# A decoder step's HGRN2 recurrence: the decayed q and k of a head multiplied in place, without a second buffer and the copies into it

## The chip, the cores and the metric

The kernel runs on one core of one Trainium2 chip. Its metric is the device time of one launch in microseconds (us). Of the kernel before, three runs are at hand: 1033.81, 1034.29 and 1036.57 us, median 1034.29. The engines of the core are named as the profile names them: PE (TensorE, matrix products; PEld is its loading of weights), DVE (VectorE), ACT (ScalarE), POOL (GpSimd) and SP (SyncE, which here only issues transfers). Each engine works through its own list of instructions in a fixed order, and semaphores make one engine wait for another.

## The reference

The kernel computes one inference step of a hybrid decoder layer of width 1024, for a prompt of 512 tokens and for 8 single new tokens (samples) with stored states, 520 columns in all. Cut to what matters here:

```
u = (rmsnorm(x) * (1 + scale1) + shift1) @ w_in          # eight parts of 1024 columns
q, f, i, og, xb, yb, ga, gb = split(u)
o_a = rmsnorm(HGRN2(silu(q), k, i, log f)) * silu(og)    # 8 heads, 128 x 128 state each
o_b = RGLRU(conv(xb)) * gelu(yb)
merged = sigmoid(ga) * (o_a @ w_branch_a) + sigmoid(gb) * (o_b @ w_branch_b)
x = x + gate1 * (merged @ w_out)
x = x + gate2 * (relu(h2 @ w_ff1) ** 2 @ w_ff2)          # and a last rmsnorm
```

HGRN2 is per head a recurrence S_t = diag(f_t) S_(t-1) + k_t v_t^T with the output o_t = S_t^T q_t. In chunks this is a triangular matrix A[t, s] = sum over the key dimension of q_t k_s times the product of the decays f between s and t, applied to v, plus the part that comes from the state at the start of the chunk. RG-LRU is an elementwise recurrence h_t = a_t h_(t-1) + sqrt(1 - a_t^2)(i_t x_t).

## The kernel before

**Products.** Every large product is done in three passes of a high and a low part: high weight by high activation, high weight by low activation, low weight by high activation (`products`, its matmul on L150). One group of 128 output columns over 1024 rows is 48 matmuls of 128x128 by 128x260. A weight tile of 512 KB comes in on SP's queue as `wst` (L102); ACT makes its high part `whi` (L111, a copy into another format) and DVE its low part `wlo`, the difference (L114). Both must be there before the group's products can be done.

**Order of the work.** A list of steps is built: for each head h of eight, `head(h)`, then two groups of the RG-LRU (`rg_x` after even heads, `rg_y` after odd ones); then the eight gate groups (`gate`, part 6 of `w_in`), in their middle `end_recurrences` and `begin_tail`, which load the heads' and the RG-LRU's results back from DRAM (`load_branches`, L877 and L882 on POOL's queue, with five buffers `t`; L200 on ACT and L201 on DVE split them into high and low parts `a` and `b`); then the products of branch a, the other gates, branch b, the output projection and the MLP. Some groups of the modulation product (L408, its result copied out by ACT at L413) are mixed in. The engines do not run these steps in program order: a planner lays out all instructions of the program over all engines with its own model of their durations, and what it decides is the order that each engine keeps. Waits follow from the data and from buffers that are used again. A few instructions, such as the reading of PSUM, have a higher priority.

**A head.** `head` makes f, k (L540) and q by activations, puts q*f, k and q into the three slots of a tile X of 128 x 3 x 520 (two buffers), and the samples' columns into `fkq`. `head_sample_v` transposes the samples' v on PE (L589), copies it (L591, DVE), writes it to DRAM (L593) and reads it back broadcast over all partitions as `vb` (L595, one buffer). `head_sample` updates the eight samples' states: ACT scales a state (L602) and DVE adds k v (L603, which waits for `vb`), for each sample; PE then makes the outputs (L609), and transposes them at L614, and DVE takes the wanted ones into `os` (L616).

**The levels of the recurrence.** `head_prompt` builds A for chunks of 128 tokens by doubling. L655 makes the diagonal products and those of the first level. A level of size b = 1, 2, 4, ..., 64 joins neighbouring blocks of b tokens: PE multiplies k of the left block by q of the right one (`block_level` L641 for b = 2 to 16, L673 for 32, L679 for 64), the result goes into the triangular matrix (`copy_predicated` into `a32`, L689, or ACT's copies into `at`), and then the q of every right block and the k of every left one, half of the columns of each, are multiplied by the block's decay (L681, 128 x 512 elements), while the decays of the level are multiplied in pairs for the next (L698). Before, L681 writes its half to a second tile Y, and a copy puts the halves that were not multiplied, as far as the other tile hasn't got them yet, there too (ACT L683 for b = 1, DVE L687 for all others); X and Y then change their names, and the next level works on the other tile.

After the last level, PE transposes k (L710) and multiplies it by v (L714), DVE chains the four chunk states (L716, L718), PE makes the outputs (L725, L727), ACT squares and sums them (L732), DVE makes the reciprocal root (L733 and L209 to L215), ACT scales (L737), PE transposes (L741), DVE multiplies by the gate (L743) and SP's queue stores the result (L744).

**RG-LRU.** `rg_x` makes gates with small block-diagonal products (L782, sigmoid L174). `rg_scans`, in odd heads for two units, is exp and tanh (L817, L818), square (L820), a combination on DVE (L821), sqrt on ACT (L824), then on DVE a product (L830) and the scan (L832). ACT loads a table before L817 and before L824.

Of the kernel before, what the change touches and what calls it, by code (L numbers as in the profile page):

```python
# [6 lines left out]
F32 = mybir.dt.float32  # L7
# [4 lines left out]
OP = mybir.AluOpType  # L12
# [6 lines left out]
T = L + NB  # L19
# [56 lines left out]
class Kernel:  # L76
# [541 lines left out]
    def head_prompt(self, h, f, X, q, v, og):  # L618
        nc = self.nc

        pv = self.pps.tile([128, 512], F32, name="ps")
        for c in range(NC):
            nc.tensor.transpose(pv[:, c * C:(c + 1) * C], v[:, c * C:(c + 1) * C], self.ident)
        vn = self.slot(self.hg, "g")
        nc.scalar.copy(vn[:, :L], pv)

        Y = self.hg.tile([128, 2, T], F32, name="Y", bufs=2)
        nc.vector.tensor_tensor(X[:, 0, :L], q[:, :L], f[:, :L], OP.mult)  # L630
        T_ = self.hg.tile([128, 508], F32, name="tb", bufs=2)
        tb, to = f[:, :L], 0
        a32 = self.hg.tile([128, NC, 32], F32, name="a32")
        at = self.at[h % 2]

        def block_level(x, y):
            p = self.pps.tile([128, 512], F32, name="ps")
            for c in range(NC):
                for j in range(4):
                    s = slice(c * C + 32 * j, c * C + 32 * j + 32)  # L640
                    nc.tensor.matmul(p[32 * j:32 * j + 32, c * 32:c * 32 + 32], x[:, s], y[:, s], start=True, stop=True)  # L641
            return p[:, :128].rearrange("p (c t) -> p c t", c=NC)

        def view(t, first_q, first_k, step, n, b):

            return bass.AP(tensor=t.tensor, offset=t.offset + first_q,
                           ap=[t.ap[0], [T + first_k - first_q, 2], [step, n], [1, b]])


        p = self.pps.tile([128, 512], F32, name="ps")  # L650
        for c in range(NC):
            for j in range(4):
                s = c * C + 32 * j
                o = p[32 * j:32 * j + 32, c * 64:c * 64 + 64].rearrange("p (x t) -> p x t", x=2)
                nc.tensor.matmul(o, X[:, 1, s:s + 32], X[:, 0::2, s:s + 32], start=True, stop=True)  # L655
        first = p[:, :256].rearrange("p (c x t) -> p c x t", c=NC, x=2)
        nc.vector.tensor_tensor(a32, first[:, :, 1], self.mdiag, OP.mult)
        b = 1
        while b < C:
            Q, K = X[:, 0], X[:, 1]  # L660

            n = L // (2 * b)
            fac = bass.AP(tensor=tb.tensor, offset=tb.offset, ap=[tb.ap[0], [1, 2], [2, n], [0, b]])
            if b == 1:
                p = first[:, :, 0]
            elif b <= 16:
                p = block_level(K, Q)
            elif b == 32:
                p = self.pps.tile([128, 512], F32, name="ps")
                for c in range(NC):  # L670
                    for j in (0, 64):
                        s = c * C + j
                        nc.tensor.matmul(p[j:j + 32, c * 32:c * 32 + 32], K[:, s:s + 32], Q[:, s + 32:s + 64],  # L673
                                         start=True, stop=True)
            else:
                p = self.pps.tile([128, 512], F32, name="ps")
                for c in range(NC):
                    s = c * C
                    nc.tensor.matmul(p[:64, c * 64:c * 64 + 64], K[:, s:s + 64], Q[:, s + 64:s + 128],  # L679
                                     start=True, stop=True)  # L680
            nc.vector.tensor_tensor(view(Y, b, 0, 2 * b, n, b), view(X, b, 0, 2 * b, n, b), fac, OP.mult)  # L681
            if b == 1:
                nc.scalar.copy(view(Y, 0, 1, 2, n, 1), view(X, 0, 1, 2, n, 1))  # L683
            else:

                h2 = b // 2
                nc.vector.tensor_copy(view(Y, h2, b, 2 * b, n, h2), view(X, h2, b, 2 * b, n, h2))  # L687
            if b <= 16:
                nc.vector.copy_predicated(a32, self.masks[b], p)  # L689
            elif b == 32:  # L690
                for j in (0, 64):
                    nc.scalar.copy(at[j:j + 32, :, j + 32:j + 64],
                                   p[j:j + 32, :128].rearrange("p (c t) -> p c t", c=NC))
            else:
                nc.scalar.copy(at[:64, :, 64:], p[:64, :256].rearrange("p (c t) -> p c t", c=NC))
            t2 = tb.rearrange("p (n two) -> p n two", two=2)
            tn = T_[:, to:to + n]
            nc.vector.tensor_tensor(tn, t2[:, :, 0], t2[:, :, 1], OP.mult)  # L698
            tb, to = tn, to + n
            X, Y = Y, X  # L700
            b *= 2
        Q, K = X[:, 0], X[:, 1]
        for j in range(0, 128, 32):
            nc.vector.tensor_copy(at[j:j + 32, :, j:j + 32], a32[j:j + 32])

        pk = self.ppt.tile([128, 512], F32, name="pt")
        for c in range(NC):
            nc.tensor.transpose(pk[:, c * C:(c + 1) * C], K[:, c * C:(c + 1) * C], self.ident)
        kn = self.slot(self.hg, "g")
        nc.scalar.copy(kn[:, :L], pk)  # L710
        pkv = self.ppt.tile([128, 512], F32, name="pt")
        for c in range(NC):
            s = slice(c * C, (c + 1) * C)
            nc.tensor.matmul(pkv[:, s], kn[:, s], vn[:, s], start=True, stop=True)  # L714
        S = self.slot(self.hg, "g")
        nc.vector.tensor_copy(S[:, :128], pkv[:, :128])  # L716
        for c in range(1, NC):
            nc.vector.scalar_tensor_tensor(S[:, c * 128:(c + 1) * 128], S[:, (c - 1) * 128:c * 128], tb[:, c:c + 1],  # L718
                                           pkv[:, c * 128:(c + 1) * 128], OP.mult, OP.add)
        nc.sync.dma_start(self.o["hgrn_p"][0, 0, h], S[:, 3 * 128:4 * 128])  # L720

        po = self.ppt.tile([128, 512], F32, name="pt")
        for c in range(NC):
            s = slice(c * C, (c + 1) * C)
            nc.tensor.matmul(po[:, s], at[:, c], vn[:, s], start=True, stop=c == 0)  # L725
            if c:
                nc.tensor.matmul(po[:, s], Q[:, s], S[:, (c - 1) * 128:c * 128], start=False, stop=True)  # L727
        o = self.slot(self.hg, "g")
        ss = self.sm.tile([128, 16], F32, name="ss")
        for c in range(NC):  # L730
            s = slice(c * C, (c + 1) * C)
            nc.scalar.activation(o[:, s], po[:, s], AF.Square, accum_out=ss[:, c:c + 1])  # L732
        nc.vector.tensor_scalar(ss[:, :NC], ss[:, :NC], 1.0 / 128, EPS, OP.mult, OP.add)  # L733
        ss = self.rsqrt_small(ss[:, :NC], NC)
        for c in range(NC):
            s = slice(c * C, (c + 1) * C)
            nc.scalar.activation(o[:, s], po[:, s], AF.Copy, scale=ss[:, c:c + 1])  # L737
        pt = self.ppt.tile([128, 512], F32, name="pt")
        for c in range(NC):
            s = slice(c * C, (c + 1) * C)  # L740
            nc.tensor.transpose(pt[:, s], o[:, s], self.ident)  # L741
        oa = og
        nc.vector.tensor_tensor(oa[:, :L], pt, og[:, :L], OP.mult)  # L743
        nc.sync.dma_start(self.oaT_d[h], oa[:, :L])  # L744
# [1128 lines left out]
```

## Time and profile before

| | |
|---|---|
| median of three runs | 1034.29 us (1033.81 to 1036.57) |
| profiled execution: span of its instructions | 1032.9 us |
| time outside the span, against the median | 1.4 us |
| PE busy | 1008.7 us, 98% |
| DVE busy | 691.4 us, 67%, 1520 instructions |
| ACT busy | 520.8 us, 50%, 988 instructions |
| heads and their recurrences | about 60 to 436 us of the span |
| first product of branch a | at 453.2 us |

The span is that of one profiled execution; no separate time of that execution is given beside it, so it is set against the median of the runs. A row of the timeline is: start in us, duration in us, engine, line and operation, output <- inputs, shape, and how many like it follow each other; in square brackets the idle time before it and what ended it. Rows that follow each other closely overlap somewhat, since an instruction's record reaches to the end of its last write; the pitch from start to start is then the shorter number. In the lists of groups the numbers behind the bar are the busy time in us, the mean of one in ns and the idle time before.

### The profile page before, as it was taken

To read this page: it belongs to the slowest core of one execution; us is meant where nothing else is said; L and a number is where in the kernel's file an instruction comes from. 1 tells how busy PE (TensorE), PEld (TensorE's weight loads), DVE (VectorE), ACT (ScalarE), POOL (GpSimd) and SP (SyncE) were. 2 spreads that over 40 slices of the span, in tenths; PEclk is the share of its full clock that TensorE was granted. 3 is DMA by queue.
4 is the path that set the end of the run, shared out by engine and by line. 5 is a ranking of instruction groups with operands and counts; after the bars stand their busy time and mean duration, and the time that the engine had idled before them with its cause. 6 is when DMAs were issued, how large, how long until landed. Compare 5 with 4: busy or idle time off the path is not lost. (4 is left out here: it accounts for less than half of the span.)

```text
span 1032.9 us, 23726 instructions
## 1 busy us (share of the span) xinstructions
PE 1008.7 (98%) x9756; PEld 967.5 (94%) x9756; DVE 691.4 (67%) x1520; ACT 520.8 (50%) x988; POOL 123.1 (12%) x228
## 2 busy tenths in 40 slices
PE   5999999999999999999999999999999999999997
PEld 2899999999999999988999999999999999999996
DVE  6787769595867869264233347667776776777685
ACT  4555744663575366342122235466555655655663
POOL 3200000000000000031000001011422231232140
PEclk9999999999999999999999999999999999999998
DMA  9673443434334324397555568322672474274242
GB/s 324 220 200 111 119 126 118 121 116 126 109 114 126 114 85 135 105 329 238 164 163 162 158 179 240 99 84 63 133 173 81 95 173 124 49 160 99 63 82 84
DMA packets 201822, 143.68 MB, mean 139 GB/s; under 512 B 6766, under 2 KB 189702, under 8 KB 201706
## 3 DMA queue, kind: packets, MB, share of 16 engines
q1 hardware_dynamic: 191090, 128.08, 41.6%
q0 software_dynamic: 10608, 14.05, 7.0%
q8 instruction: 76, 1.25, 0.5%
q14 instruction: 32, 0.26, 0.1%
q10 hardware_dynamic: 16, 0.03, 0.0%
HBM read 123.61 MB, written 11.26 MB: 131 GB/s over the span
## 5 line engine op out<-in xcount | busy, mean ns | idle before, releaser
L150 PE MATMUL mm<-h,whi 128*128 128x260 f32 (+1 forms) x2944 | 490.3, 286 | 0.0
L150 PEld LDWEIGHTS mm<-h,whi 128*128 128x128 f32 x2944 | 409.7, 189 | 5.2 <-issue 4.1
L150 PE MATMUL mm<-h,wlo 128*128 128x260 f32 x1472 | 305.2, 286 | 0.1
L111 ACT CAST whi<-wst 128x1024 fp32r<-128x1024 f32 x164 | 171.7, 1048 | 221.6 <-PE mm L150 182.0
L114 DVE TENSOR_TENSOR wlo<-wst,whi 128x1024 fp32r<-128x1024 f32 x164 | 200.3, 1223 | 102.0 <-ACT whi L111 100.3
L150 PEld LDWEIGHTS mm<-h,wlo 128*128 128x128 f32 x1472 | 230.5, 189 | 1.9 <-issue 0.8
L150 PE MATMUL mm<-a,whi 128*128 128x260 f32 x512 | 85.3, 286 | 0.0
L150 PEld LDWEIGHTS mm<-a,whi 128*128 128x128 f32 x512 | 70.5, 188 | 3.8 <-issue 3.3
L150 PE MATMUL mm<-a,wlo 128*128 128x260 f32 x256 | 51.7, 283 | 0.0
L877 POOL DMA_DIRECT2D t<-oaT_d x8 | 4.4, 552 | 387.8 <-ACT sq L750 378.1
L1270 DVE TENSOR_TENSOR f<-f 128x260 f32<-128x260 f32 x64 | 27.4, 428 | 27.6 <-ACT f L1265 26.9
L1259 ACT ACTIVATE ft<-ft,fsh 128x512 f32<-128x512 f32 (+2 forms) x36 | 24.0, 675 | 36.1 <-DVE ft L1256 36.1
L150 PE MATMUL mm<-b,whi 128*128 128x260 f32 x256 | 41.9, 286 | 0.0
L1262 POOL TENSOR_TENSOR ft<-ft,fsh 128x8 f32<-128x8 f32 x28 | 18.4, 657 | 187.3 <-DVE ft L1256 187.3
L150 PEld LDWEIGHTS mm<-a,wlo 128*128 128x128 f32 x256 | 39.5, 188 | 0.0
L150 PEld LDWEIGHTS mm<-b,whi 128*128 128x128 f32 x256 | 35.0, 188 | 3.3 <-issue 2.5
L1304 POOL DMA_DIRECT2D ma<-snap x28 | 26.8, 972 | 38.3 <-issue 29.2
L1286 POOL DMA_DIRECT2D ma<-snap x28 | 25.9, 926 | 36.7 <-DMA ma<-snap 25.1
L893 DVE TENSOR_TENSOR t<-mm,t 128x520 f32<-128x520 f32 x8 | 5.6, 700 | 36.5 <-PE mm L150 36.5
L1265 ACT ACTIVATE f<-ft 128x520 f32<-128x520 f32 (+1 forms) x36 | 20.7, 587 | 15.0 <-POOL ft L1263 13.0
L602 ACT ACTIVATE st<-st,fkq 128x128 f32<-128x128 f32 x64 | 20.2, 391 | 14.8 <-DVE fkq L581 12.5
L150 PE MATMUL mm<-b,wlo 128*128 128x260 f32 x128 | 25.9, 284 | 0.0
(579 smaller groups left out, 1940.9 us busy)
## 6 DMA issues: line engine op xcount, KB each, us to landing
wst<-in_w_in_dram SPq DMA_DIRECT2D x64, 512.0 KB
wst<-in_w_mod_dram SPq DMA_DIRECT2D x32, 512.0 KB
wst<-in_w_ff_dram SPq DMA_DIRECT2D x64, 256.0 KB
wst<-in_w_ff_dram SPq DMA_DIRECT2D x32, 512.0 KB
wm<-in_w_mod_dram SPq DMA_DIRECT2D x16, 512.0 KB
st<-in_state_hgrn_dram SPq DMA_DIRECT2D x8, 512.0 KB
vb<-vd SPq DMA_DIRECT2D x8, 512.0 KB
out_dram<-st SPq DMA_DIRECT2D x8, 512.0 KB
```

Source lines behind the costliest of these rows:

```text
L111: ins = self.nc.scalar.copy(hi, st)
L114: self.nc.vector.tensor_tensor(lo, st, hi.bitcast(F32), OP.subtract)
L150: self.last_product = self.nc.tensor.matmul(ps[s][:, :c.stop - c.start], x, y[:, c], start=first and n == 0, stop=last and n == 2)
L602: nc.scalar.activation(st[:, b], st[:, b], AF.Copy, scale=fkq[:, 0, b:b + 1])
L877: nc.gpsimd.dma_start(t[:, :L], self.oaT_d[h])
L893: self.nc.vector.tensor_tensor(self.two(s), ps, self.two(s), OP.mult)
L1259: nc.scalar.activation(t[:, :p], t[:, :p], AF.Relu, bias=sh[:, 0:1])
L1262: eng.tensor_tensor(t[:, p:], t[:, p:], sh[:, 1:9], OP.add)
L1265: nc.scalar.activation(f, self.two(self.ft)[:, a:a + n], AF.Square)
L1270: self.nc.vector.tensor_tensor(f[:, n], f[:, a], f[:, b], op)
L1286: nc.gpsimd.dma_start(x[1][:, b], v[:, :n], accum_op=OP.add)
L1304: nc.gpsimd.dma_start(x[t][:, a], s[p], accum_op=OP.add)
```

## The change

The tile Y goes. At each level the multiplication by the decays reads and writes the same half of X, and it is issued behind the step that takes the level's products into the triangular matrix instead of ahead of it. The copies of the other halves on ACT and DVE are not needed, since they never leave X, and X and Y no longer change places. Nothing else in the program text is different; the planner lays the changed program out anew.

```
-        Y = self.hg.tile([128, 2, T], F32, name="Y", bufs=2)
         nc.vector.tensor_tensor(X[:, 0, :L], q[:, :L], f[:, :L], OP.mult)
...
-            nc.vector.tensor_tensor(view(Y, b, 0, 2 * b, n, b), view(X, b, 0, 2 * b, n, b), fac, OP.mult)
-            if b == 1:
-                nc.scalar.copy(view(Y, 0, 1, 2, n, 1), view(X, 0, 1, 2, n, 1))
-            else:
-
-                h2 = b // 2
-                nc.vector.tensor_copy(view(Y, h2, b, 2 * b, n, h2), view(X, h2, b, 2 * b, n, h2))
             if b <= 16:
                 nc.vector.copy_predicated(a32, self.masks[b], p)
             elif b == 32:
...
             else:
                 nc.scalar.copy(at[:64, :, 64:], p[:64, :256].rearrange("p (c t) -> p c t", c=NC))
+            half = view(X, b, 0, 2 * b, n, b)
+            nc.vector.tensor_tensor(half, half, fac, OP.mult)
             t2 = tb.rearrange("p (n two) -> p n two", two=2)
             tn = T_[:, to:to + n]
             nc.vector.tensor_tensor(tn, t2[:, :, 0], t2[:, :, 1], OP.mult)
             tb, to = tn, to + n
-            X, Y = Y, X
             b *= 2
```

More of the change, by code (lines that the diff above doesn't have):

```diff
@@ L625, in head_prompt @@
         nc.scalar.copy(vn[:, :L], pv)
-        Y = self.hg.tile([128, 2, T], F32, name="Y", bufs=2)
         nc.vector.tensor_tensor(X[:, 0, :L], q[:, :L], f[:, :L], OP.mult)
@@ L680, in head_prompt @@
                                      start=True, stop=True)
[L681 to L687, printed above, removed]
             if b <= 16:
@@ L695, in head_prompt @@
                 nc.scalar.copy(at[:64, :, 64:], p[:64, :256].rearrange("p (c t) -> p c t", c=NC))
+            half = view(X, b, 0, 2 * b, n, b)
+            nc.vector.tensor_tensor(half, half, fac, OP.mult)
             t2 = tb.rearrange("p (n two) -> p n two", two=2)
@@ L699, in head_prompt @@
             tb, to = tn, to + n
-            X, Y = Y, X
             b *= 2
```

## Prediction

> **What bounds the kernel.** The page comes first: how busy each engine is and at what clock.
>
> ```profile
> span 1032.9 us, 23726 instructions
> PE 1008.7 (98%) x9756; PEld 967.5 (94%) x9756; DVE 691.4 (67%) x1520; ACT 520.8 (50%) x988; POOL 123.1 (12%) x228
> PEclk9999999999999999999999999999999999999998
> ```
>
> PE is the bound, at a full clock. Work that leaves DVE or ACT shortens nothing by itself; only a place where PE stands still can gain or lose. So the second view is a stretch with nothing but products (its columns: window, length, busy time of PE, PEld, DVE, ACT, POOL, mean clock, DMA share, GB/s), and the third the list of what PE and DVE waited for (total, times, longest).
>
> ```profile
> 650.00:675.00 25.00, 25.00 (x210) 25.00 (x209) 16.78 (x37) 11.50 (x17) 0.00 (x0) 1.00 0.30 85
> PE ps L641 <- DVE X L687: 1.5, 1, 1.5
> PE pt L614 <- DVE e L743: 1.2, 2, 1.0
> DVE st L603 <- DMA vb<-vd: 8.5, 6, 3.6
> ```
>
> 210 products in 25.00 us are 0.119 us each: PE's pace, by which I turn a count of products into time. In the heads' stage (60 to 430 us) PE lost only 2.7 us, in the two PE rows. One of them names a copy that this change removes, so I looked at the place, first as PE and then as DVE has it.
>
> ```profile
> 251.59 0.28 PE L150 MATMUL mm<-h,wlo 128*128 128x260 f32 x1
> 253.39 0.27 PE L641 MATMUL ps<-X 128*32 128x32 f32 x8 [1.52 <-DVE X L687]
> 253.89 0.44 PE L614 MATMUL pt<-ident,sev 128*128 128x128 f32 x2 [0.23 <-DVE e L743]
> ```
> ```profile
> 243.65 0.28 DVE L591 COPY vs<-ps 8x128 f32<-8x128 f32 x1
> 247.90 0.30 DVE L689 COPY_PREDICATED a<-mask,ps 128x128 f32<-128x128 uint8 x1
> 251.81 1.14 DVE L603 SCALAR_TENSOR_TENSOR st<-vb,fkq,st 128x128 f32<-128x128 f32 x4 [3.61 <-DMA vb<-vd]
> 252.86 0.39 DVE L687 COPY X<-Y 128x256 f32<-128x256 f32 x1
> ```
>
> The copy L687 that PE waited for was ready to go at 248.2. It was late because on DVE, which runs in the planned order, it stood behind four L603, and these wait for vb, a transfer through DRAM that began when L591 ended (243.93) and landed at 251.8: 7.9 us. The copy cost PE something through its place in the queue, not through its length. That is the pattern I look for in the changed order.
>
> **The change, part by part.** What goes:
>
> ```profile
> L687 DVE COPY X<-Y 128x256 f32<-128x256 f32 x24 | 7.9, 328 | 0.0
> L687 DVE COPY Y<-X 128x256 f32<-128x256 f32 x24 | 7.1, 298 | 0.0
> L683 ACT COPY Y<-X x8: 657/668/690, 66.5 to 370.2; 128x512 f32<-128x512 f32 x8
> L681 DVE TENSOR_TENSOR X<-Y,tb 128x512 f32<-128x512 f32 x24 | 16.6, 690 | 0.1
> ```
>
> 1. Removed: 48 copies on DVE (7.9 + 7.1 = 15.0 us) and 8 on ACT (8 x 0.668 = 5.3 us). Both lie beside PE's products: gain on the path 0. The 56 multiplications stay as they were in size; written in place they take the same 0.69 us (bounds: 0 to 0.1 us each, as X<-Y and Y<-X differ by 3 ns), so 0. PE's instructions are the same in number.
>
> 2. The old stalls: 1.5 + 1.2 and some 0.5 of small ones fall away if nothing else is late there: -3.2 us (bounds -3.2 to 0). Both come from places that the new order moves apart.
>
> 3. A new dependence: the multiplication of a level overwrites what the level's own block products read, so it can't start until they have read it, and the next level's products wait for it. That chain is 0.5 (32 block products, below) + 0.30 (L689, ahead of it on DVE) + 0.69 + two handovers between engines of 0.1, my estimate, about 1.7 us; the changed order leaves 30 to 40 products (3.6 to 4.8 us) between one level's block products and the next. Cost 0; without that cover each level would cost up to 1.7.
>
> 4. The order. The planner has put the instructions of all engines from 60 to 470 us anew (PE's first 415 and last 4460 of 8618 stand as before). Within each pair of heads the end of the recurrence is drawn out: from L589, the first of a head's transposes, to L741, its last, there stood 454 PE instructions and now 665. Three places come out of this.
>
> 4a. The boundary of a pair of heads (h = 3, 5, 7), where the RG-LRU's exp, tanh and sqrt run. Before:
>
> ```profile
> 286.04 0.28 ACT L732 ACTIVATE g<-pt 128x128 f32<-128x128 f32 x1 [1.44 <-PE pt L727]
> 286.96 0.22 ACT L732 ACTIVATION_READ_ACCUMULATOR g<-pt 128x1 f32 x1
> 293.55 0.59 ACT L625 COPY g<-ps 128x512 f32<-128x512 f32 x1 [0.96 <-PE ps L623]
> 294.24 0.48 ACT L174 ACTIVATE gate<-pb,pa 128x260 f32<-128x260 f32 x1
> 299.58 1.04 ACT L111 CAST whi<-wst 128x1024 fp32r<-128x1024 f32 x1
> 301.12 1.28 ACT L824 ACT_TABLE_LOAD   x1
> 302.41 0.64 ACT L824 ACTIVATE xc<-xc 128x520 f32<-128x520 f32 x1
> ```
> ```profile
> 300.83 1.14 DVE L603 SCALAR_TENSOR_TENSOR st<-vb,fkq,st 128x128 f32<-128x128 f32 x4
> 302.49 0.70 DVE L681 TENSOR_TENSOR Y<-X,tb 128x512 f32<-128x512 f32 x1
> 303.10 1.23 DVE L114 TENSOR_TENSOR wlo<-wst,whi 128x1024 fp32r<-128x1024 f32 x1
> 306.46 1.23 DVE L832 TENSOR_TENSOR_SCAN hs<-ag,gate 128x512 f32<-128x512 f32 x1
> ```
>
> L114 makes the low half of the next weights, without which PE can't go on; it stood ahead of both L830 and the scan. The changed order (lines as numbered before) is:
>
> ```
> ACT: L174 | table, L817 x2, L818, L820, L818, L820 | L732 x4 | L625 | table, L824 ...
> DVE: L603, L830 <-sqrt, L603 x3, small, L603 x2, L830, L603 x2, L832 scan, 2 small, L114
> ```
>
> L114 now stands behind the first L830, so behind a sqrt. ACT from the last gate's sigmoid to the end of that sqrt: 299.58 - 294.24 = 5.34 up to the last square; L732 1.14; L625 0.55; table and sqrt 1.92; together 8.95. Then DVE, by the pitch from start to start (0.28 for L603, 0.61 for rows of 0.70, 1.14 for L114 and the scan): 2 x 0.61 + 7 x 0.28 + 0.3 of small ones + 1.14 + 1.23 = 5.85. With 0.35 for the handovers, an estimate, the products have their weights 15.1 us after the gate's last matmul. PE's work in that time is 88 products (10.5) and 45 small matmuls, priced from the rows of such groups:
>
> ```profile
> 292.92 0.60 PE L623 MATMUL ps<-ident,e 128*128 128x128 f32 x4
> 295.67 0.65 PE L655 MATMUL ps<-X 128*32 128x64 f32 x32
> 296.14 0.48 PE L641 MATMUL ps<-Y 128*32 128x32 f32 x32
> ```
>
> L655 and L641 take 0.5 each by their pitch; L623, the output products and the rest about 2.1: 3.1, so 13.6 us in all. PE stands 1.5 to 1.6 us. I take 1.6, three times: 4.8 (bounds 0.8, if ACT starts early, to 2.4, if vb is late as at 251.8).
>
> 4b. Head 1's boundary: the last transposes L741 wait for a scaling on ACT that waits for DVE's rsqrt chain, which stands behind eight L603 and their vb. The nearest price is that of 4a; I take 1.5 us (0.5 to 2.5).
>
> 4c. Heads 2, 4, 6: all eight L603 now stand ahead of L657 and the first multiplication, and PE has 59 products and 28 small matmuls between L589 and the first L641, about 9.8 us. The chain is 0.5 (L589, L591), vb's landing, 8 x 0.28, 0.2 (L657), 0.69 and 0.1: 3.7 plus the landing, so one of up to 6.1 us is covered and the 7.9 of above would cost 1.8. Of the six waits for vb, 8.5 us in all, the longest was that one with 3.6; the other five average 1.0, so those landings were some 2.6 us shorter, 5.3 us as an estimate. I take 0.6 for the three heads together, a late one in three (0 to 2.5).
>
> 4d. Into branch a:
>
> ```profile
> 435.76 0.38 PE L614 MATMUL pt<-ident,sev 128*128 128x128 f32 x2
> 444.42 0.63 ACT L200 CAST a<-t 128x520 fp32r<-128x520 f32 x1 [4.74 <-DVE t L878]
> 453.20 0.75 PE L150 MATMUL mm<-a,whi 128*128 128x260 f32 x4
> 454.86 0.54 POOL L882 DMA_DIRECT2D t<-obT_d  x1 [1.12 <-DVE a L201]
> 462.02 0.63 ACT L200 CAST b<-t 128x520 fp32r<-128x520 f32 x1 [1.89 <-DMA t<-obT_d]
> 462.55 1.05 ACT L111 CAST whi<-wst 128x1024 fp32r<-128x1024 f32 x1
> 470.00 0.37 ACT L413 COPY modev<-pt 128x256 f32<-128x256 f32 x1
> t<-obT_d POOLq DMA_DIRECT2D x8, 260.0 KB, 6.1
> ```
>
> Head 7's last matmul L614 now stands 113 products ahead of the first of branch a, not 164: 51 x 0.119 = 6.1 us less of the 8.8 us that lay between a's first cast and its use. Two things are then late. The sixth cast of a stands on ACT behind L413, which waits for eight L408 that PE does right before the product wanting that cast: 0.25 + 0.37 + 0.63, PE stands 1.25. And the weights of the fourth product group (L111) stand behind the cast of the third b, whose load waits on POOL until the sixth a has left its buffer: low half 0.7, issue 0.3, transfer 6.1, cast 0.63, L111 1.05, together 8.8, against 40 products (4.8) on PE: 4.0. Together 5.2 (bounds: the third b took 462.02 - 454.86 = 7.2 here, which gives 6.3; a load hidden altogether leaves the 1.25). I take the median of the group, as this load is one of the same eight.
>
> The stores L720 and L744 move with the end of each recurrence on SP's queue, past weight loads issued ahead of their use; the list of waits has no product that waited for such a load in this stage, so 0 (bounds 0 to 1).
>
> The Trainium skill ("SBUF — State Buffer", The DMA setup-cost knee) prices a transfer at about 2 us fixed plus its bytes over the bandwidth; an estimate from that page is 2.6 us for such a load. Here the same transfer shows 6.1, so the measurement decides; by the Trainium skill's price 4d would be 1.7 and the sum 3.5 lower.
>
> Sum: 4.8 + 1.5 + 0.6 + 5.2 - 3.2 = +8.9 us. The profiled execution's span is 1032.9, 1.4 under the median of the runs, 1034.29; the difference is outside the steps, so 1034.3 + 8.9 = 1043.2.
>
> **The rivals.**
>
> - Faster. The vb transfers land under 6.1 us and the handovers at the boundaries are 1.6 us shorter than I count, so DVE, 15 us lighter, is early everywhere and the old 3.2 us go: 1031.1. It is decided by L114 at the boundaries: if its end comes within 13.6 us of the gate, it holds. For it: DVE is 67% busy. Against it: the scan and two L830 stand ahead of L114 in the order, and no lighter DVE changes that. Chance 0.05.
> - No difference that can be measured (0.3%, 3.1 us, is what the runs of this kernel can tell from none). The new waits are real but at their lower ends (2.4 + 0.5 + 0 + 1.25 - 3.2 = +1.0: 1035.3), or only one of 4a and 4d is there (up to +2.9). The old order had the same kinds of waits and paid only 3.2. Chance 0.17.
> - A bubble at each level. If PE waited for the multiplication in place at all 56 levels, 0.3 us each would be 17 us: 1051. For it: the chain of step 3 is new. Against: 3.6 us of cover for 1.7. Chance 0.06. The Trainium skill ("Perfetto Trace Analysis", Optimization Strategy) reads gaps that repeat on the engine that should be saturated as too few buffers, which speaks against giving up Y; the trace of before, with Y, has one gap at L641 in its 32 levels.
>
> **How the numbers follow.** My forecast (boundaries and branch a, +4 to +13 us) has 0.72, its rivals 0.05, 0.17 and 0.06. Low end: all lower bounds give the +1.0 above. High end: all upper ones give 7.2 + 2.5 + 2.5 + 6.3 - 3.2 = +15.3 at once; +13.7 leaves some 1 in 10 above it, the bubbles among them. Range 1035 to 1048. Faster by 0.3% 0.05, within it 0.17, slower 0.78.
>
> **What would show it.** Right: PE idle before L150 with L114 as releaser near 220, 300 and 390 us, over 1 us each; PE idle near 460 us after L111 or L200, with a b load behind it; no idle before L641 by L681 at more than a few levels; DVE 15 us less busy. Wrong: a PE at those places without gaps, a landing of vb or b that differs by 2 us or more from the above, or gaps at L641 in every head.

## The result and the profile after

The changed kernel takes 1046.87 us (median; 1046.27 to 1049.15) against 1034.41 us before (1033.81 to 1036.57, four runs of each): a ratio of 1.0121 (95% interval 1.0107 to 1.0136), 12.5 us slower. The forecast was 1043.2 us. The profiled execution of the changed kernel is its slowest, 1049.15 us: its span is 14.4 us longer than that of before, and 1.4 us of this are lost behind the last matmul of L150, in the MLP and the last norm, whose instructions the change leaves as they were.

In the changed kernel's lines, the multiplication is L689 (L681 before), L641 and L655 are L640 and L654, L689 is L681, L830 and L832 are L823 and L825, L737 and L741 are L730 and L734, L865 is L858; L114, L150, L408, L603 and L614 keep their numbers. The page and the list of PE's waits (total, times, longest), rows of the start left out:

```profile
span 1047.4 us, 23650 instructions
PE 1015.8 (97%) x9756; PEld 972.2 (93%) x9756; DVE 674.4 (64%) x1472; ACT 516.2 (49%) x980; POOL 123.2 (12%) x228
PEclk9999999999999999989999999999999999999998
...
PE pt L408 <- DMA wst<-in_w_mod_dram: 4.8, 1, 4.8
...
PE mm L150 <- DVE wlo L114: 3.5, 3, 2.0
...
PE pt L734 <- ACT g L730: 1.1, 1, 1.1
...
PE mm L150 <- ACT a L200: 1.0, 1, 1.0
PE mm L150 <- ACT whi L111: 0.3, 1, 0.3
```

DVE is 17.0 us less busy and ACT 4.6, and the two old waits, for the copy L687 and at L614, are gone. In their place stand a wait of 4.8 us for a weight transfer, three waits of 3.5 us in all for low halves of weights, and three single ones. PE is 7.1 us *busier* with the same matmuls, and one slice of its clock shows an 8.

Where the time went can be read by the same matmul of L150, counted from its first, in both traces:

```
matmul of L150, counted from 0       before     after    later by
0                                      53.8      53.9       0.1 us
2451 (the heads are over)             438.5     443.2       4.7 us
2688 (in branch a)                    477.1     489.8      12.7 us
3072                                  530.1     543.1      13.0 us
5615 (the last)                       976.0     989.0      13.0 us
```

At 2451 the changed kernel still has six transposes of head 7 to do (four L734 and two L614, some 0.5 us); otherwise both have done the same work. So 5.1 us of the loss lie in the heads, 7.8 us between there and 3072, around the entry into branch a, and nothing between there and the last matmul of L150. Where the cut lies matters: a few products later, at 2496, the difference is only 2.4 us, but the kernel before has by then also done 24 matmuls L408 and two L752 (2.7 us), which the changed kernel does behind it.

**The boundary of heads.** First PE, then DVE, then ACT around the longest of the three waits, at head 3:

```profile
212.24 0.65 PE L150 MATMUL mm<-h,whi 128*128 128x260 f32 x4
214.90 0.51 PE L150 MATMUL mm<-h,wlo 128*128 128x260 f32 x2 [2.02 <-DVE wlo L114]
```
```profile
208.96 0.35 DVE L603 SCALAR_TENSOR_TENSOR st<-vb,fkq,st 128x128 f32<-128x128 f32 x1 [2.01 <-DMA vb<-vd]
...
212.36 1.22 DVE L825 TENSOR_TENSOR_SCAN hs<-ag,gate 128x512 f32<-128x512 f32 x1
...
213.63 1.22 DVE L114 TENSOR_TENSOR wlo<-wst,whi 128x1024 fp32r<-128x1024 f32 x1
```
```profile
205.89 1.28 ACT L817 ACT_TABLE_LOAD   x1
207.18 1.17 ACT L817 ACTIVATE xc<-xc 128x520 f32<-128x520 f32 x2
208.26 1.03 ACT L111 CAST whi<-wst 128x1024 fp32r<-128x1024 f32 x1
```

This is the queue of the prediction's step 4a: L114 last, behind the states, the product with the sqrt and the scan. At head 3 it was vb that held it up: DVE waited 2.0 us for it, until 209.0, and the sqrt (L817) was over at 208.4. At heads 5 and 7 it was the sqrt, for which DVE waited 0.5 and 0.9 us, and PE stood for 0.65 and 0.84 us. DVE and then PE at head 5:

```profile
302.96 0.70 DVE L823 TENSOR_TENSOR gate<-gate,xc 128x520 f32<-128x520 f32 x1 [0.52 <-ACT xc L817]
```
```profile
308.65 0.51 PE L150 MATMUL mm<-h,wlo 128*128 128x260 f32 x2 [0.65 <-DVE wlo L114]
```

At head 3 the loss does not end with the wait. The windows of 1 us behind it (last columns: granted clock, DMA share, GB/s):

```profile
215.00:216.00 1.00, 1.00 (x9) 1.00 (x10) 1.00 (x3) 0.43 (x1) 0.00 (x0) 1.00 0.24 71
216.00:217.00 1.00, 1.00 (x8) 1.00 (x7) 1.00 (x2) 1.00 (x2) 0.00 (x0) 0.53 0.53 130
217.00:218.00 1.00, 1.00 (x6) 1.00 (x6) 1.00 (x6) 0.63 (x2) 0.00 (x0) 0.50 1.07 323
219.00:220.00 1.00, 1.00 (x36) 0.94 (x33) 1.00 (x3) 0.07 (x1) 0.00 (x0) 0.77 0.00 0
```

PE is back at work from 214.9, but from 216.1 to 219.5 its clock is halved, and products follow each other at 0.217 us instead of 0.119: 3.4 us of work at 55% of the pace, some 1.5 us more. In such stretches a PE with the same instructions becomes busier.

**The entry into branch a.** PE, and the windows of 2 us beside it:

```profile
458.31 0.94 PE L858 MATMUL ps<-ident,xlast 128*11 128x128 f32 x7
464.02 1.08 PE L408 MATMUL pt<-wst,cT 128*32 128x256 f32 x8 [4.77 <-DMA wst<-in_w_mod_dram]
```
```profile
459.00:461.00 2.00, 0.25 (x3) 0.00 (x0) 1.13 (x2) 0.00 (x0) 0.58 (x2) 1.00 1.09 367
461.00:463.00 2.00, 0.00 (x0) 0.00 (x0) 0.00 (x0) 0.24 (x1) 0.49 (x1) 0.70 1.01 394
465.00:467.00 2.00, 2.00 (x14) 1.60 (x11) 2.00 (x5) 1.44 (x3) 0.99 (x2) 0.50 0.52 104
```

PE waits for a weight of the modulation product. SP's queue and the median landing of such loads say why:

```profile
445.17 0.38 SPq L102 DMA_DIRECT2D wst<-in_w_branch_a_dram  x1
...
451.51 0.33 SPq L100 DMA_DIRECT2D wst<-in_w_mod_dram  x1
452.82 0.38 SPq L102 DMA_DIRECT2D wst<-in_w_branch_a_dram  x1
454.13 1.10 SPq L100 DMA_DIRECT2D wst<-in_w_mod_dram  x2
```
```profile
wst<-in_w_mod_dram SPq DMA_DIRECT2D x32, 512.0 KB, 4.6
```

The load was issued at 454.13, when a buffer came free, and landed at 464.0: 9.8 us where the median is 4.6. With it four loads of a, two of x and three other weights were under way, and the DMA engines were full (share over 1.0). Behind the wait the clock was halved until 468.6.

### The profile page after: what moved, and what is told of

It reads as the page before. It is cut to its first block, busy times and chain, and to the rows that moved or that the text cites. A ratio compares the mean times of both kernels' runs of the same rounds, so it can differ in the third digit from the quotient of the medians.

```text
span 1047.4 us, 23650 instructions
## 1 busy us (share of the span) xinstructions
PE 1015.8 (97%) x9756; PEld 972.2 (93%) x9756; DVE 674.4 (64%) x1472; ACT 516.2 (49%) x980; POOL 123.2 (12%) x228
## 3 DMA queue, kind: packets, MB, share of 16 engines
q8 instruction: 76, 1.25, 0.5%
## 5 line engine op out<-in xcount | busy, mean ns | idle before, releaser
L150 PE MATMUL mm<-h,whi 128*128 128x260 f32 (+1 forms) x2944 | 490.3, 286 | 0.0
L150 PEld LDWEIGHTS mm<-h,whi 128*128 128x128 f32 x2944 | 409.7, 189 | 5.5 <-issue 4.3
L150 PE MATMUL mm<-h,wlo 128*128 128x260 f32 x1472 | 305.0, 286 | 3.5 <-DVE wlo L114 3.5
L114 DVE TENSOR_TENSOR wlo<-wst,whi 128x1024 fp32r<-128x1024 f32 x164 | 200.0, 1221 | 123.1 <-ACT whi L111 121.8
L111 ACT CAST whi<-wst 128x1024 fp32r<-128x1024 f32 x164 | 171.7, 1049 | 206.2 <-PE mm L150 170.7
L150 PEld LDWEIGHTS mm<-h,wlo 128*128 128x128 f32 x1472 | 230.6, 189 | 5.5 <-DVE wlo L114 4.1
L150 PE MATMUL mm<-a,whi 128*128 128x260 f32 x512 | 85.3, 287 | 1.3 <-ACT a L200 1.0
L150 PEld LDWEIGHTS mm<-a,whi 128*128 128x128 f32 x512 | 70.8, 189 | 5.1 <-ACT a L200 1.5
L150 PE MATMUL mm<-a,wlo 128*128 128x260 f32 x256 | 52.0, 283 | 0.0
L150 PE MATMUL mm<-b,whi 128*128 128x260 f32 x256 | 41.8, 285 | 0.0
L150 PEld LDWEIGHTS mm<-a,wlo 128*128 128x128 f32 x256 | 39.5, 188 | 0.0
L689 DVE TENSOR_TENSOR X<-X,tb 128x512 f32<-128x512 f32 x48 | 32.8, 684 | 8.2 <-PE ps L678 7.4
L150 PEld LDWEIGHTS mm<-b,whi 128*128 128x128 f32 x256 | 35.0, 188 | 3.3 <-issue 2.5
L603 DVE SCALAR_TENSOR_TENSOR st<-vb,fkq,st 128x128 f32<-128x128 f32 x64 | 18.2, 347 | 24.3 <-DMA vb<-vd 24.2
```

The source lines that it names most:

```text
L111: ins = self.nc.scalar.copy(hi, st)
L114: self.nc.vector.tensor_tensor(lo, st, hi.bitcast(F32), OP.subtract)
L150: self.last_product = self.nc.tensor.matmul(ps[s][:, :c.stop - c.start], x, y[:, c], start=first and n == 0, stop=last and n == 2)
L603: nc.vector.scalar_tensor_tensor(st[:, b], vb[:, b], fkq[:, 1, b:b + 1], st[:, b], OP.mult, OP.add)
L689: nc.vector.tensor_tensor(half, half, fac, OP.mult)
```

## The experiments

Where the order of instructions was to be held or changed by hand, each engine's list was laid down as it stood in one of the two kernels, with this, shortened here, at the end of the build (mine: an engine's instructions as the program text issues them); waits, buffers and data stay those of the program:

```
+def lay(tc):                       # ORDER: one list of positions per engine
+    for engine, order in ORDER.items():
+        for x, y in zip(order, order[1:]):
+            tc.add_manual_dep(mine[engine][y], mine[engine][x].name, NOSYNC, reason="order")
```

The theory after the result: the multiplication in place costs nothing by itself where it stands, the new order costs 12.5 us, at the boundaries and at the entry into branch a. The rival: the new dependence costs at every level.

**The new data flow in the old order, and the old data flow in the new order.**

```
 after.py, ORDER = before's lists, without the copies; L689 directly behind L681 of its level
```

> The multiplications in place, without Y and the copies, but every engine's instructions in the order of the kernel before (each multiplication directly behind the step that takes its level's products). Theory 'order': the change costs through the new order alone, so this is no slower than before; the old wait of 1.5 us at L641 behind L687 goes: 1031.5 to 1034.5 us. Rival 'dependence': the multiplication that overwrites what the level's products read costs at each level: 1040 us or more.

```
 before.py, ORDER = after's lists; each L687 directly behind its L681
```

> The kernel before with Y and all its copies, but every engine's instructions in the order of the changed kernel (each copy of DVE directly behind its multiplication, the copy of ACT where the first multiplication began in the trace). Theory 'order': as slow as the changed kernel, or slower by the copies at the boundaries: 1045 to 1050 us. Rival 'dependence': about 1034 us.

The first took 1060.23 us, ratio 1.0252 (1.0235 to 1.0268), the second 1054.5 us, ratio 1.0203 (1.0184 to 1.0223). The theory fell with the first: in the old order the new data flow costs 26 us. The second lies 4.5 us above its range, and its rival fell too. The first run's list of PE's waits, then PE and DVE in head 0:

```profile
PE ps L640 <- DVE X L689: 15.3, 6, 6.1
```
```profile
68.27 0.65 PE L654 MATMUL ps<-X 128*32 128x64 f32 x32
75.06 0.65 PE L640 MATMUL ps<-X 128*32 128x32 f32 x32 [6.13 <-DVE X L689]
```
```profile
72.97 1.14 DVE L603 SCALAR_TENSOR_TENSOR st<-vb,fkq,st 128x128 f32<-128x128 f32 x4 [1.77 <-DMA vb<-vd]
74.03 0.29 DVE L681 COPY_PREDICATED a<-mask,ps 128x128 f32<-128x128 uint8 x1
74.23 0.68 DVE L689 TENSOR_TENSOR X<-X,e 128x512 f32<-128x512 f32 x1
```

L654 makes the first level's products, L640 the second's. Before, the first multiplication wrote to Y and did not have to wait for L655, and PE could go from one to the other at once. In place it must come after L654's reading, and L640 after it. All eight heads wait at the first L640, 1.4 to 6.1 us each and 19.1 us in all (two of the waits, of 2.3 and 1.4 us, stand in the list under other names), and none waits at a later L640.

Not all of this is the price of the dependence. The run puts the multiplication behind the copy L681 of its level; in the kernel before, and in the changed kernel too, the first level's stands ahead of that copy. In heads 0, 1 and 3 of the old order the copy stands behind four L603, which wait for vb, as the rows of head 0 show: these three heads have 10.3 of the 19.1 us, and all three stretches of halved clock that follow. In heads 2, 4 and 6 DVE has next to nothing in between, and PE waits 1.43 us in each, within the 1.7 us of step 3. If heads 0, 1 and 3 waited no longer than these, some 6 us of waits and 5 us of halved clock would go, so some 15 of the 26 us is an estimate for the dependence itself in this order. A run with the first multiplication ahead of the copy was not made.

The products of L150 that each order has between one level's matmuls and the next show what the planner did about the dependence:

```
          1-2  2-4  4-8  8-16  16-32  32-64  64-transposes
before h=2   0   35   27    21     28     33    15
       h=5   0   36   46    37     26     33     0
after  h=2  40   29   36    34     23     29    18
       h=5  28   58   38    35     28     30    29
```

So the cover of 30 to 40 products of step 3 is real: between the first two levels 28 to 41 products stand where there were 0 or 14. With it each head is stretched (from the first transpose to the last, 442 to 498 instructions in PE's list before, 519 to 691 after). That the planner stretched the heads to get this cover is an inference; the run below that takes the first level out of place bears on it. With the copies in that stretched order the kernel is slower still, by 7.6 us; the waits at L114, 3.5 us in the changed kernel, are

```profile
PE mm L150 <- DVE wlo L114: 6.7, 3, 2.4
```

Neither data flow is good in the other's order.

**Which level it is.**

```
+        Y = self.hg.tile([128, 2, T], F32, name="Y", bufs=2)
...
+            if b == 1:   # ahead of copy_predicated
+                nc.vector.tensor_tensor(view(Y, 1, 0, 2, n, 1), view(X, 1, 0, 2, n, 1), fac, OP.mult)
+                nc.scalar.copy(view(Y, 0, 1, 2, n, 1), view(X, 0, 1, 2, n, 1))
...
+            if b > 1:
                 nc.vector.tensor_tensor(half, half, fac, OP.mult)
+            else:
+                X = Y
```

The program ran once with ORDER = before's lists without DVE's copies, and once with no ORDER:

> Only the first level is multiplied from X into Y, with the copy of ACT; the levels from 2 on are multiplied in place in Y, and DVE's 48 copies are gone. Every engine in the order of the kernel before. Theory 'first level': of the 26 us that the change cost in that order, the first level's products cost nearly all, since PE has no products between L655 and the first L641 there; the levels from 2 on have 14 to 61 products between them and cost under 2 us, mostly where PE goes from L679 to L708 at once; with the old wait at L641 gone: 1032 to 1035.5 us. Rival 'every level': 1040 us or more.

> The same program with the order that the planner gives it. Its heads are nearly as short as before (459 to 531 PE instructions from the first to the last transpose but for head 1 with 668, against 442 to 498 before and 519 to 691 in the changed kernel), while head 7 ends 52 products ahead of branch a (before 114, changed 47). Theory: the waits at the boundaries mostly go, those at the entry into branch a stay: 1040 to 1045 us. Rival: both went with the stretched heads: 1033 to 1037 us.

In the old order this took 1039.45 us, ratio 1.0049 (1.0025 to 1.0073): 21 of the 26 us belong to the first level, to its dependence and its place in DVE's list together, and some 5 are left (the five runs lie between 1037.1 and 1043.4), between the two theories. The waits are spread:

```profile
PE ps L641 <- DVE Y L694: 3.5, 6, 0.9
...
PE pt L614 <- DVE e L743: 1.0, 1, 1.0
PE pt L708 <- DVE Y L694: 0.9, 2, 0.5
```

With the planner's order it took 1042.56 us, ratio 1.0083 (1.0067 to 1.0100). By matmul 2451 and the same six transposes its heads take as long as before, though waits at two boundaries remain, and the entry into branch a costs 8.6 us. (The 3.2 us that the expectation for the run with all three cures takes from here compare matmul 2496, by which the kernel before has done 2.7 us more of other work.) So with the first level out of place the heads are short again but for head 1, which supports the inference, while head 7's tail is as late as in the changed kernel. The heads and the entry are two matters, and why the planner puts that tail so near to branch a stays open.

```profile
PE pt L408 <- DMA wst<-in_w_mod_dram: 4.9, 1, 4.9
PE mm L150 <- DVE wlo L114: 3.4, 2, 2.0
```

**The boundaries alone.**

```
 after.py, ORDER = after's lists, but at h = 3, 5, 7
 ACT:  L111 (whi)  ahead of the sqrt's table load   (was behind both sqrt)
 DVE:  L114 (wlo)  ahead of the first L823          (was behind the first scan)
```

> The changed kernel in its own order, but at the boundaries of heads 3, 5 and 7 the next weights' high part (ACT, L111) stands ahead of the sqrt and its table load, and their low part (DVE, L114) ahead of the first L830 (lines as before). Theory: the three waits of 2.0, 0.8 and 1.0 us by L114 go, and with the first of them the stretch of 3.3 us behind it in which the clock is halved (1.5 us): 1041 to 1042.5 us. Rival: the sqrt, the scan or the states that are now later make PE wait as long elsewhere: 1045 us or more.

1043.27 us, ratio 1.0089 (1.0074 to 1.0104), 3.6 us less than the changed kernel and 0.8 us above the range of the theory. No wait at L114 is left, and the clock stays whole in the heads, but a wait of 0.6 us at L640 is new. For the same work the heads take 0.4 us longer than in the kernel before: without these waits the change loses almost nothing there, and it does not gain the 3.2 us that step 2 promised either.

```profile
PE pt L408 <- DMA wst<-in_w_mod_dram: 4.7, 1, 4.7
...
PE pt L734 <- ACT g L730: 1.1, 1, 1.1
```

**The entry into branch a.** Two causes were held against each other: staging buffers filled with modulation weights that PE could not use yet, and a late tail of the last head.

```
-            if m > TAIL:
-                mod_step()
...
-            mod_step(2 if m <= TAIL else 1)
+            mod_step(2)
```

> The changed kernel with the four modulation groups among the last gates moved in among the products of branch a. Theory 'staging': at the entry into branch a the weights came late because three of the four staging buffers held modulation weights whose products stood behind head 7's last transposes; with that the wait of 4.8 us, some 2.2 us of halved clock and the wait of 1.0 us for the cast behind L413 go, and about 1 us is left until the first a is there: 1038 to 1041 us. Rival of the prediction's step 4d: the third b's load ahead of L111 then makes PE wait 4 us: 1043 to 1047 us.

```
+        for m in range(2):
+            one("w_in", 56 + m, lambda m: gb.update({m: self.gate(7, m, self.slot(self.abb, "gb"))}), m)
         for m in range(KO):
             if m == 2:
                 steps.append(([], self.rg_out))
...
+            if m > 1:
                 one("w_in", 56 + m, lambda m: gb.update({m: self.gate(7, m, self.slot(self.tail, "t"))}), m)
```

> The changed kernel with two of the eight groups of part 7's gates (96 products, 11.4 us of PE) moved ahead of the products of branch a; the order of the heads is the same. Theory 'late tail': the entry into branch a costs 10 us because head 7's last transposes stand some 67 products (8 us) nearer to it than before, and the sample columns, the buffers of the weights and their loads are late with them; with 11.4 us of other products between, nearly all of it goes: 1036.5 to 1039.5 us. Rival 'crowded transfers': the loads of a, b and the weights fall together at the entry whatever stands before it, and PE waits for them as long: 1044 us or more.

With the modulation later it took 1045.0 us, ratio 1.0106 (1.0089 to 1.0124): a miss. The time lies in the rival's range, but not for the rival's reason: the wait only moved. The modulation weights, now others, were again loaded as the buffers came free, and PE could use them 6.2 and 6.3 us after their issue.

```profile
PE pt L408 <- DMA wst<-in_w_mod_dram: 5.2, 2, 3.3
```

With the gates ahead it took 1038.37 us, ratio 1.0042 (1.0028 to 1.0056), 8.5 us less than the changed kernel, as expected of the late tail; the control below shows how much of this moving the gates brings without the change. The wait for the weights is gone from the list:

```profile
PE mm L150 <- DVE wlo L114: 2.7, 4, 0.9
...
PE pt L734 <- ACT g L730: 1.1, 1, 1.1
```

**Both cures, and all three.**

```
 the program with two groups of gates ahead of branch a, ORDER = its own lists,
 L111 and L114 at h = 3, 5, 7 moved as in the experiment on the boundaries
```

> The same, and at the boundaries of heads 3, 5 and 7 the weights' high and low part ahead of sqrt and L830, as in the experiment on the low half. Theory: the two costs are apart and add up, -3.6 us beside the one before: 1032.5 to 1036 us, about the time of the kernel before, with the multiplications in place and none of the old waits of 1.5 and 1.0 us. Rival: the two are one cost seen in two places, and the second cure brings under 1 us.

1035.95 us, ratio 1.0014 (1.0005 to 1.0024): the cures add up to 10.9 of the 12.5 us. The second brings 2.4 us beside the first and not the 3.6 it brought alone.

```
 the program with the first level out of place, gates ahead of branch a
 (range(2), and range(1) in the second run), ORDER = its own lists,
 L111 and L114 at h = 5, 7 moved likewise
```

> First level out of place (planned order), two groups of gates ahead of branch a, and at the boundaries of heads 5 and 7 the weights' halves ahead of sqrt and L830. Theory: the three cures add up; the heads, 3.2 us shorter than before in the planned run, lose 4 more, and the entry into branch a no longer costs: 1029.5 to 1033 us, faster than both kernels. Rival: what the heads gain is given back where branch a begins, as with the gates moved alone: 1033.5 to 1037 us.

> The same with one group of gates (48 products, 5.7 us) ahead of branch a: head 7's last transposes are then 100 products from it, 114 in the kernel before. Theory 'late tail': enough cover, within 1 us of the run with two groups. Rival: the five loads of a, the weights and the modulation still meet and PE waits 2 us or more: 1034 us or more.

1032.21 us with two groups, ratio 0.998 (0.9971 to 0.9988), and 1034.07 us with one, ratio 1.0001 (0.9991 to 1.0011). The first is faster than both kernels; its longest wait of PE between the start and the last norm is 1.1 us. The second is a miss: it is 1.9 us above the first where 1 us was allowed, and the entry still waits, for the copying out of rows of the RG-LRU and for a:

```profile
PE ps L865 <- DVE rows L867: 1.8, 1, 1.8
...
PE mm L150 <- ACT a L200: 0.8, 1, 0.8
```

**The control.** The gates moved in the kernel before, with Y and all copies:

```
 before.py with the edit of the gates, no ORDER
```

> The kernel before, with Y and all copies, and two groups of gates moved ahead of branch a: the control for the kernel that beat both. Theory: the kernel before waits nowhere at the entry into branch a, so cover there is worth nothing, and it keeps its old waits of 1.5 and 1.0 us in the heads: 1033.5 to 1036 us, and the 2.3 us of the faster kernel come from the heads. Rival: moving the gates is itself worth the 2.3 us: 1031 to 1033 us.

1032.55 us, ratio 0.9989 (0.9978 to 1.0): the rival holds. Moving the gates is worth 1.7 us without the change (the interval just reaches no gain at all); in the profiled executions, by pairs of matmuls, PE turns three times less from L150 to L408 and back, which accounts for 1.6 us. One wait of the heads is not there either, though PE, DVE and ACT keep the order of the kernel before up to head 7's end: the one of 1.5 us at L641 in head 4.

```profile
250.17 1.14 DVE L603 SCALAR_TENSOR_TENSOR st<-vb,fkq,st 128x128 f32<-128x128 f32 x4 [1.81 <-DMA vb<-vd]
```
```profile
251.96 0.27 PE L641 MATMUL ps<-X 128*32 128x32 f32 x8
```

Here vb landed 6.1 us after L591, in the profiled execution of the kernel before 7.9. So this wait was a matter of one execution's landing, and not of the order alone.

Against this control the change with both cures (ratio 1.0014, 1.0005 to 1.0024) is still some 3 us slower. The fastest kernel, which keeps the first level out of place (0.998, 0.9971 to 0.9988), is level with the control. So what it has over the kernel before cannot be credited to the multiplication in place: nothing here shows a gain from that change.

## Why the prediction was right, and where it was not

The direction and the range held (1035 to 1048, measured 1046.87); the sum of +8.9 us was 3.6 too small. By the table above, the heads cost 5.1 us where steps 4a to 4c less step 2 gave 3.7, and the entry 7.8 us where step 4d gave 5.2. The high end of the range was added up with the old stalls gone in full; with its own bound of 0 for them it would have been 3.2 us higher.

Step 1 priced the copies at 0. In the changed order they are not free: with them it takes 7.6 us more, as L114 is later still. Step 2 was right that both old waits go, but not that their 3.2 us are won: the longer of them is missing in the control as well, which keeps the order, and the heads gained nothing even with the waits at L114 cured.

Step 3 priced the new dependence at 0 because the changed order covers it. PE has no wait at L640 on the changed kernel's list, so the price was right, but the reading was short: the cover was taken as given, and what it takes to get it was not asked. "The order" of step 4 is, in the heads, probably the cost of step 3.

Step 4a had its three places and the place of L114 in the queue right, shown by the experiment that moves L111 and L114. From the start of the gate's last matmul to the delayed product it took 15.0 us at head 5 and 15.2 at head 7, against a chain of 15.1; at head 3, with vb late, 16.4. It said 3 x 1.6 us; the waits were 2.0 and two that share 1.5, and a halved clock added 1.5: 5.0 against 4.8. That the sums agree is partly chance, as the clock was not foreseen. Step 4b said 1.5, and 1.1 was measured, with L730 as releaser. Step 4c said 0.6, and PE has no wait there on the list; vb landed 5.7 to 6.1 us after L591 in these heads, just within the 6.1 that it counted as covered.

Step 4d failed in part: 5.2 us forecast, 7.8 measured, and most of that by another way. The cast behind L413 is there, 1.0 for 1.25. The other 4.0 us, L111 behind the third b, did not happen: PE waited 0.3 us for an L111 in the whole kernel. What happened, a wait of 4.8 us for a weight and the halved clock behind it, was excluded by the paragraph behind it, that the loads on SP's queue cost 0 (bounds 0 to 1). The buffers they need came free as late as head 7's tail, and the loads met those of a. That the total stayed within the range is here luck. There is a slip in the working as well: 113 and 164 are instructions of PE from L741; from L614 it is 47 products after and 114 before, 8.0 us less and not 6.1, nearly all of the 8.8 us of slack, which should have made the whole entry suspect rather than one cast.

Of the rivals, the bubble at each level did not come in the changed kernel. The first experiment shows it in the old order, but at the first level alone. As for the price of a transfer, the load that decided was not the one priced at 6.1 us but one of 512 KB, and it took 9.8.

## What to carry to other kernels

A second buffer may look like waste when its copies are off the critical path, but it also cuts a dependence between engines: before removing it, count what work the bounding engine has between the two ends of that dependence in the order as it stands, above all where there is none. Where a planner lays out the program, ask what it will stretch to hide the new dependence, and who waits for the end of what is stretched. When a loss is split between stages, cut both traces where the same work is done; the count of one kind of product does not tell that. And when a moved instruction is put into an old order by hand, look at what it now stands behind. Last, look for waits that follow from a stage being late as a whole (buffers not yet free, loads that now meet) and not only for the one instruction that stands in the wrong place.

## What the runs showed of the hardware

A short wait of PE can cost more than its length. Gaps are counted here from the start of one matmul to the start of the next, between the first product and the MLP, in the profiled executions of all the kernels above. No gap of up to 1.8 us was followed by a halved clock; of eleven gaps from 2.1 to 2.7 us five were; and all six of 3.5 us or more were. The clock goes to 0.50 between 2.8 and 4.4 us behind the start of the gap, and for a gap of 2.1 to 2.7 us it comes back 3.4 us on, at a price of about 1.5 us. Gaps of the same length go both ways: the new data flow in the old order had 2.56 us with and 2.71 us without it.

The Trainium skill ("TensorE: Matmul & The Clock Gate", What's actually happening) says that the clock is halved after an idle window of about 3.4 us, and that these windows run freely. The length of the halved stretch agrees with such a window, and windows that run freely would explain why equal gaps differ; no run here tests that. That a whole window must be idle, as that sentence can be read, does not agree, since a gap of 2.3 us, of which PE was idle for 2.0, was enough at 212.6 in the changed kernel.

A transfer of 512 KB that lands in 4.6 us as a median took 9.8 when it met the loads of a, of x and of other weights.
